# Squares of two RMS norms summed by TensorE, the normalised input split without being made, and 12 of the first 16 modulation tiles as matrix products with the weights moving

## The chip, the cores and the metric

The kernel runs on one core of one Trainium2 chip. A core has five engines that each work through their own list of instructions in order and wait for one another by semaphores: TensorE (PE, matrix products), VectorE (DVE), ScalarE (ACT), GpSimd (POOL) and SyncE (SP, which here only starts DMA transfers). The metric is the device time of one execution in microseconds (us).

## The reference, cut to what matters

Two blocks follow each other on 256 tokens of width 1024. The first has two layers; each runs a token mixer over 256 context tokens and 256 latent tokens, and then a PEER feed-forward layer. Both read a modulated RMS norm of the residual stream x:

```python
def rms_norm(x, g):
    y = xf * lax.rsqrt(jnp.mean(xf * xf, axis=-1, keepdims=True) + EPS)
    return (y * g)
def modulate(h, shift, scale):
    return h * (1 + scale) + shift
...
mod_x = (cond_x @ w_mod[l] + b_mod[l])      # 6 * 1024 values: shift, scale, gate, twice
hx  = modulate(rms_norm(x, norm1_g[l]), sh1x, sc1x)   # before the mixer: h @ w_in
hx2 = modulate(rms_norm(x, norm2_g[l]), sh2x, sc2x)   # before PEER: h @ wq (its queries)
```

The second block (feed-forward, retention and attention, feed-forward, twice) is not touched by the change.

## The kernel before, in words

x is kept transposed in SBUF: 128 partitions hold 128 channels, `x[:, k, :]` is the k-th of 8 channel blocks, and its 512 columns are the tokens (256 context, 256 latent). A projection is a sum over the 8 blocks; each f32 factor is cut in two parts, hi and lo (type fp32r), and three products replace one: hi·hi, lo·hi, hi·lo (`mm3`, L246 to L248). For weights, `Stream` fetches 512 KB tiles by DMA into six `raw` buffers; ScalarE writes `whi` (L209), VectorE or GpSimd `wlo` (L210). The order of the tiles is written out in `plan`, and SP issues their DMAs in that order: the seventh waits until the first buffer is free. `take` hands out the next tile; with `more` set it first splits further tiles, up to two ahead, as far as the buffers reach.

There are four norms of this kind: before the mixer of layer 0 (`mixer_start`), before PEER of layer 0, before the mixer of layer 1, and before PEER of layer 1 (the last with 256 tokens). Each goes so. `square_sum` squares one block of x on ScalarE and adds it to `nsum` on GpSimd or VectorE, block after block, as the residual (`resid`, L875) makes x. `norm_rstd` sums `nsum` over the partitions on TensorE (L333: for each 128 tokens a product with `nsum` as the stationary factor and a column of ones moving), takes the power -1/2 on GpSimd (L291) and spreads it over the partitions (L311, `n_pb`). `norm_tile` multiplies x by `n_pb` (VectorE, L346), writes `hhi` by ScalarE (L349) and the same value h in f32 by GpSimd or ScalarE (L353, L351), and VectorE takes `hlo` = h - `hhi` (L354). `norm_split` runs this block by block, with the first two projections behind each block.

At the start x comes in by DMA, and the first norm needs 16 modulation columns (8 scales, 8 shifts, for context and latent), each the product of a 512 KB tile of `w_mod` and the two condition vectors. `MODE` says who makes a tile: "T" (6 tiles) TensorE with the tile stationary and the two vectors moving, 8 products of 2 columns (L406); "V" (8 tiles) VectorE, two passes of 1024 elements with a running sum (L719); "G" (2 tiles) GpSimd and ScalarE (L714, L715).

PEER of layer 0 (`phase_v`) ends with eight PSUM banks `y`. `last(db)` adds what was gathered for 128 tokens by a product with the unit matrix (L1564), then comes the residual into x (L875) and the square for the next norm. In the output projection of a mixer, `proj` makes block m (24 products), then `resid`, `square_sum` and, in layer 0, one or two modulation tiles on VectorE.

Of the kernel before, what the change touches and what calls it, by code (L numbers as in the profile page):

```python
# [9 lines left out]
F32 = mybir.dt.float32  # L10
# [6 lines left out]
ALU = mybir.AluOpType  # L17
# [4 lines left out]
L = 2  # L22
# [84 lines left out]
def _host(inp):  # L107
# [8 lines left out]
    wt = g["w_mod"].reshape(L, KD, 128, 48, 128).transpose(0, 3, 2, 1, 4).reshape(L, 48, 128, 1024)  # L116
    wr = g["w_mod"].reshape(L, 1024, 48, 128).transpose(0, 2, 3, 1)
    a["w_modt"] = np.stack([(wt if MODE[i:i + 1] == "T" else wr)[l, m] for i, (l, m) in enumerate(MODT)])
# [120 lines left out]
class Build:  # L239
# [73 lines left out]
    def square_sum(self, pool, k, t0, eng=None, sq=None):  # L313

        nc, xk = self.nc, self.x[:, k, t0:]
        acc = self.nsum[:, t0:]
        if k == 0:
            nc.scalar.activation(acc, xk, AF.Square)
            return
        if sq is None:  # L320
            sq = pool.tile([128, 512], F32, name="n_sq", tag="n_sq", bufs=2)
        sq = sq[:, t0:]
# [3 lines left out]
    def norm_rstd(self, pool, psp, tag, t0):  # L326


        nb = (T - t0) // 128
        st = psp.tile([128, 512], F32, name="n_st", tag=tag)  # L330
        for tb in range(nb):
            s = slice(t0 + tb * 128, t0 + tb * 128 + 128)
            self.nc.tensor.matmul(st[:, tb:tb + 1], self.nsum[:, s], self.ones, start=True, stop=True)  # L333
        r = self.rsqrt_cols(pool, st[:, :nb], nb, 1.0 / 1024)
        pb = psp.tile([128, 512], F32, name="n_pb", tag=tag)
        for tb in range(nb):
            self.bcast(pb[:, tb * 128:tb * 128 + 128], r[:, tb:tb + 1])
        return pb

    def norm_tile(self, pool, k, pb, segs, t0, hhi, hlo, act=False):  # L340


        nc, N = self.nc, T - t0
        t, h = (pool.tile([128, w], F32, name="n_t", tag=g, bufs=2)
                for w, g in zip(self.norm_widths, ("n_t", "St")))
        nc.vector.tensor_mul(t[:, :N], self.x[:, k, t0:], pb[:, :N])  # L346
        for sl, g, sh in segs:
            ps = slice(sl.start - t0, sl.stop - t0)
            nc.scalar.activation(hhi[:, k, ps], t[:, ps], AF.Identity, scale=g(k), bias=sh(k))  # L349
            if act:  # L350
                nc.scalar.activation(h[:, ps], t[:, ps], AF.Identity, scale=g(k), bias=sh(k))  # L351
            else:
                nc.gpsimd.tensor_scalar(h[:, ps], t[:, ps], g(k), sh(k), op0=ALU.mult, op1=ALU.add)  # L353
        return lambda: nc.vector.tensor_sub(hlo[:, k, :N], h[:, :N], hhi[:, k, :N])  # L354

    def norm_split(self, pool, psp, tag, segs, t0, hhi, hlo, names, banks, ready=None):


        pb = self.norm_rstd(pool, psp, tag, t0)
# [16 lines left out]
    def mixer_start(self, p, pp, sp, hhi, hlo):  # L376
# [18 lines left out]
        segs = self.segs(0, 0, 0)  # L395

        def mods(k):
            mv = self.modv[0]
            src = [mv[:, 8 + k], mv[:, k]]
            for i in range(2):  # L400
                mode = MODE[2 * k + i]
                if mode == "T":
                    w = S.take(("modt", 2 * k + i), False)
                    src[i] = mo[:, 2 * k + i]
                    for kd in range(KD):
                        nc.tensor.matmul(src[i], w[:, kd * 128:kd * 128 + 128], cc[:, kd], start=kd == 0,  # L406
                                         stop=kd == KD - 1)
                else:
                    self.mod_tile(p, cb, 2 * k + i, "att" if mode == "G" else "sg", mode == "G", False)
            return src  # L410

        def gains(k, src):
            nc.vector.tensor_scalar(self.gsc[0][0][:, k], src[0], b1[:, k:k + 1],
                                    self.col["n1"][:, 0, k:k + 1], op0=ALU.add, op1=ALU.mult)
            nc.vector.tensor_scalar_add(self.modv[0][:, k], src[1], b[:, k:k + 1])

        made = {0: mods(0)}
        for k in range(KD):
            self.square_sum(p, k, 0, nc.vector)
        made[1] = mods(1)  # L420
        pb = self.norm_rstd(p, pp, "pp", 0)
        us = [S.take(("in", 0, j), False) for j in range(3)]
        nc.vector.tensor_scalar_add(b1, b[:, 8:16], 1.0)
        late = None
        for k in range(2, KD + 3):
            if k < KD:
                made[k] = mods(k)
            nxt = None
            if k - 2 < KD:
                gains(k - 2, made.pop(k - 2))  # L430
                nxt = self.norm_tile(p, k - 2, pb, segs, 0, hhi, hlo, True)
            if late:
                late()
                d = k - 3
# [78 lines left out]
    def plan(self):  # L513
# [1564 lines left out]
```

## Time and profile before

| | |
|---|---|
| time, median of 3 runs | 3865.55 us (3859.89 to 3867.29) |
| the profiled execution | 3849.67 us, of which its span 3847.7 us |
| busy: TensorE, VectorE, ScalarE, GpSimd | 95%, 75%, 49%, 31% of the span |
| chain that ended last: TensorE, VectorE, ScalarE, DMA | 74%, 13%, 5%, 3% of the span |
| last product of the first three projections issued | 74.44 us after the span's start |
| last column of the norm's sums, layer 0 to 1 (end of PEER) | 1675.54 us |

The first and the last instruction bound the span; the time holds about 2 us more. The profiled execution lies 16 us below the median of the runs. Busy shares are averages over stages; the chain follows, from the last instruction back, what released each step. The duration of a product contains its way through the array, so that two neighbours overlap: their pace is the distance of their starts.

### The profile page before, as it was taken

What the parts mean: (1) busy time and instruction counts of PE and PEld (TensorE: products, weight loads), DVE (VectorE), ACT (ScalarE), POOL (GpSimd) and SP (SyncE); (2) the same over time, 40 slices, a digit from 0 to 9 for tenths busy, and PEclk for the clock granted to TensorE, in tenths of its full rate; (3) what the DMA queues carried; (4) which work ended last, traced back from release to release, by engine and by line L of the source; (5) the groups of instructions that cost most, each with busy time, mean ns of one, the idle gap of its engine ahead of it and who ended that gap; (6) DMA issues with size and microseconds to landing.
All of it is one profiled execution on the core that took longest, in us unless ns stands there. A gap on an engine that the chain in (4) does not pass through costs nothing.

```text
span 3847.7 us, 67340 instructions
## 1 busy us (share of the span) xinstructions
PE 3662.7 (95%) x25755; PEld 3492.3 (91%) x25755; DVE 2893.2 (75%) x5232; ACT 1898.9 (49%) x3480; POOL 1181.2 (31%) x1126
## 2 busy tenths in 40 slices
PE   6898999999989999988899999999999999999999
PEld 5787799989889999978899999999999799998799
DVE  7977888898879999969687775876665566655555
ACT  5323347575744433343448685544445454444444
POOL 2433414343466676624470501212000300001300
PEclk9999999999999999989999999999999999999899
DMA  5423357989899999943366867878555255553254
GB/s 215 142 67 126 105 172 273 323 289 324 287 352 368 372 368 365 358 140 117 131 180 206 272 199 243 300 236 259 180 185 162 78 170 183 177 184 129 78 182 152
DMA packets 289121, 831.86 MB, mean 216 GB/s; under 512 B 32469, under 2 KB 98389, under 8 KB 287749
## 3 DMA queue, kind: packets, MB, share of 16 engines
q1 hardware_dynamic: 220782, 594.67, 46.7%
q0 software_dynamic: 67296, 231.65, 16.8%
q8 instruction: 201, 3.29, 0.4%
q10 hardware_dynamic: 720, 1.25, 0.1%
q14 instruction: 122, 1.00, 0.1%
HBM read 760.40 MB, written 67.04 MB: 215 GB/s over the span
## 4 chain that ended last, share of the span: by engine, by line
PE 74%; DVE 13%; ACT 5%; DMA 3%; issue 3%; POOL 2%; SPq 0%; DVEq 0%; ACTq 0%; POOLq 0%
PE ps L246 13%; PE ps L248 13%; PE ps L247 13%; PE y L246 9%; PE y L248 9%; PE y L247 9%; DVE wlo L210 3%; ACT whi L209 1%; DVE modt L719 1%; DMA x<-in_v_rows,eidx 1%; PE gp L1401 1%; POOL wlo L210 1%; DVE acc L1279 1%; PE gp L1402 1%; DMA raw<-in_w_modt 1%
## 5 line engine op out<-in xcount | busy, mean ns | idle before, releaser
L210 DVE TENSOR_TENSOR wlo<-raw,whi 128x1024 fp32r<-128x1024 f32 x884 | 1086.4, 1232 | 561.0 <-ACT whi L209 553.5
L209 ACT ACTIVATE whi<-raw 128x1024 fp32r<-128x1024 f32 x952 | 998.7, 1052 | 444.3 <-issue 178.5
L246 PE MATMUL ps<-hhi,whi 128*128 128x256 f32 (+1 forms) x3368 | 1026.8, 305 | 10.9 <-ACT hhi L349 5.3
L248 PE MATMUL ps<-hhi,wlo 128*128 128x256 f32 (+1 forms) x3368 | 1010.3, 300 | 13.9 <-DVE wlo L210 8.1
L247 PE MATMUL ps<-hlo,whi 128*128 128x256 f32 (+1 forms) x3368 | 1010.2, 300 | 4.9 <-DVE hlo L449 4.1
L246 PEld LDWEIGHTS ps<-hhi,whi 128*128 128x128 f32 x3368 | 656.2, 195 | 42.7 <-issue 9.9
L248 PEld LDWEIGHTS ps<-hhi,wlo 128*128 128x128 f32 x3368 | 655.1, 195 | 35.7 <-DVE wlo L210 11.7
L247 PEld LDWEIGHTS ps<-hlo,whi 128*128 128x128 f32 x3368 | 655.6, 195 | 27.5 <-DVE hlo L449 8.2
L246 PE MATMUL y<-wh,whi 128*128 128x256 f32 (+1 forms) x1280 | 374.7, 293 | 14.7 <-ACT wh L509 14.7
L248 PE MATMUL y<-wh,wlo 128*128 128x256 f32 (+1 forms) x1280 | 374.3, 292 | 0.6 <-DVE wlo L210 0.6
L247 PE MATMUL y<-wl,whi 128*128 128x256 f32 (+1 forms) x1280 | 374.6, 293 | 0.0
L246 PE MATMUL ps<-h2hi,whi 128*128 128x384 f32 x1024 | 350.2, 342 | 5.9 <-ACT scs L1115 4.9
L248 PE MATMUL ps<-h2hi,wlo 128*128 128x384 f32 x1024 | 344.7, 337 | 4.3 <-DVE wlo L210 4.3
L247 PE MATMUL ps<-h2lo,whi 128*128 128x384 f32 x1024 | 343.7, 336 | 0.0
L248 PE MATMUL y<-h2hi,wlo 128*128 128x384 f32 x768 | 257.5, 335 | 1.4 <-DVE wlo L210 1.2
L246 PE MATMUL y<-h2hi,whi 128*128 128x384 f32 x768 | 257.0, 335 | 0.0
L247 PE MATMUL y<-h2lo,whi 128*128 128x384 f32 x768 | 256.9, 334 | 0.0
L246 PEld LDWEIGHTS y<-wh,whi 128*128 128x128 f32 x1280 | 242.3, 189 | 15.2 <-ACT wh L509 15.2
L248 PEld LDWEIGHTS y<-wh,wlo 128*128 128x128 f32 x1280 | 242.2, 189 | 0.9 <-DVE wlo L210 0.9
L247 PEld LDWEIGHTS y<-wl,whi 128*128 128x128 f32 x1280 | 242.1, 189 | 0.5 <-DVE wl L510 0.5
L210 POOL TENSOR_TENSOR wlo<-raw,whi 128x1024 fp32r<-128x1024 f32 x68 | 174.5, 2579 | 213.1 <-ACT whi L209 212.9
L1202 ACT ACTIVATE act<-ps 128x384 f32<-128x384 f32 (+1 forms) x236 | 104.4, 442 | 262.3 <-PE ps L248 125.0
(448 smaller groups left out, 7576.4 us busy)
## 6 DMA issues: line engine op xcount, KB each, us to landing
raw<-in_pu SPq DMA_DIRECT2D x256, 512.0 KB
raw<-in_pv SPq DMA_DIRECT2D x256, 512.0 KB
raw<-in_ffn_gu SPq DMA_DIRECT2D x176, 512.0 KB
raw<-in_w_modt SPq DMA_DIRECT2D x96, 512.0 KB
raw<-in_w_in SPq DMA_DIRECT2D x88, 512.0 KB
raw<-in_ffn_dn SPq DMA_DIRECT2D x88, 512.0 KB
gd<-stage SPq DMA_DIRECT2D x48, 512.0 KB
actd<-act POOLq DMA_DIRECT2D x125, 192.0 KB
```

What stands on the lines that cost most here:

```text
L209: self.nc.scalar.activation(hi[:, :w], raw, AF.Copy)
L210: (self.lo_eng or self.nc.vector).tensor_sub(lo[:, :w], raw, hi[:, :w])
L246: mm(ps, whi, xhi, start=first, stop=False, **kw)
L247: mm(ps, whi, xlo, start=False, stop=False, **kw)
L248: mm(ps, wlo, xhi, start=False, stop=last, **kw)
L719: self.nc.vector.scalar_tensor_tensor(t, w, 1.0, cv, op0=ALU.mult, op1=ALU.mult, accum_out=acc)
L1202: nc.scalar.activation(act, ps[:, :N], AF.Gelu)
L1279: nc.vector.scalar_tensor_tensor(self.acc, v, c, self.acc, op0=ALU.mult, op1=ALU.add)
L1401: nc.tensor.matmul(ps[:, i], B[:, :, i], Ah[:, i], start=True, stop=False)
L1402: nc.tensor.matmul(ps[:, i], B[:, :, i], Al[:, i], start=False, stop=True)
```

## The change

- `square_sum` no longer adds on VectorE or GpSimd. It squares on ScalarE and returns `add`: for each 128 tokens a product with the square stationary and ones moving, summed over the 8 blocks in PSUM (`n_st`). In the output projections `add` of block m is called after `proj` of block m + 1, at the start and in `phase_v` at once. `norm_rstd` is called at the end of the stage that makes x, `norm_along` (the spreading) where it was.
- `norm_tile`: VectorE makes x · gain · `n_pb` in two halves of 256 columns, ScalarE adds the shift for `hhi`, and VectorE makes `hlo` = (t + shift) - `hhi` in two halves. h itself, and GpSimd's and ScalarE's part in it, are gone.
- At the start four scale tiles are "V" and twelve tiles are laid out so that the two condition vectors are stationary and the weights move: two products of 512 columns in plain f32 for a tile, four tiles for a group of four columns (`modp`), a copy by ScalarE (`modrow`) and four small transposes (`columns`). The V tiles are now taken with `more` at its default, True.
- The eight first modulation tiles stand ahead of the three `in` tiles in `plan` (four did).

```diff
-MODT = ([(0, m) for k in range(8) for m in (8 + k, k)] + [(0, m) for m in range(16, 48)]
-        + [(1, m) for m in range(48)])
+FIRST = [8, None, None, 9, None, None, 10, 11] + [None] * 8
+GROUPS = (0, 12, 4)
+MODT = [(0, m) for m in FIRST] + [(0, m) for m in range(16, 48)] + [(1, m) for m in range(48)]
-MODE = "TVTVGVTVTVGVTVTV"
...
-    def square_sum(self, pool, k, t0, eng=None, sq=None):
+    def square_sum(self, pool, st, k, t0, sq=None):
...
-        nc.scalar.activation(sq, xk, AF.Square)
-        (eng or (nc.vector if k == KD - 1 else nc.gpsimd)).tensor_add(acc, acc, sq)
+        nc.scalar.activation(sq[:, :T - t0], self.x[:, k, t0:], AF.Square)
+
+        def add():
+            for tb in range((T - t0) // 128):
+                nc.tensor.matmul(st[:, tb:tb + 1], sq[:, tb * 128:tb * 128 + 128], self.ones,
+                                 start=k == 0 and tb == 0, stop=k == KD - 1, skip_group_check=True)
+        return add
...
-    def norm_tile(self, pool, k, pb, segs, t0, hhi, hlo, act=False):
+    def norm_tile(self, pool, k, pb, segs, t0, hhi, hlo):
...
-        nc.vector.tensor_mul(t[:, :N], self.x[:, k, t0:], pb[:, :N])
+        for sl, ps, g, sh in cut:
+            nc.vector.scalar_tensor_tensor(t[:, ps], self.x[:, k, sl], g(k), pb[:, ps],
+                                           op0=ALU.mult, op1=ALU.mult)
+        for sl, ps, g, sh in cut:
+            nc.scalar.activation(hhi[:, k, ps], t[:, ps], AF.Identity, bias=sh(k))
+
+        def low():
+            for sl, ps, g, sh in cut:
+                nc.vector.scalar_tensor_tensor(hlo[:, k, ps], t[:, ps], sh(k), hhi[:, k, ps],
+                                               op0=ALU.add, op1=ALU.subtract)
+        return low
...
+        def mods(n):
+
+            if FIRST[n] is not None:
+                self.mod_tile(p, cb, n, "sg", False)
+                return
+            g, u = divmod(FIRST[:n].count(None), 4)
+            w = S.take(("modt", n), False)
+            if u == 0:
+                made[g] = g1.tile([128, 512], F32, name="modp", tag="g1")
             for i in range(2):
...
+                nc.tensor.matmul(made[g][:2], cc[:, 2 * u + i], w[:, i * 512:i * 512 + 512],
+                                 start=u + i == 0, stop=u + i == 4)
+            if u == 3:
+                nc.scalar.activation(row[:2, g], made[g][:2], AF.Copy)
...
+        mods(0)
...
         for k in range(KD):
...
+            self.square_sum(p, st, k, 0)()
+            if k in (1, 3):
+                mods(1 + k // 2)
+        mods(3)
+        mods(4)
+        self.norm_rstd(st, 0)
+        mods(5)
+        pb = self.norm_along(pp, "pp", 0)
+        columns(0)
+        mods(6)
+        mods(7)
         us = [S.take(("in", 0, j), False) for j in range(3)]
...
+                if k < 4:
+                    mods(8 + 2 * k)
+                    mods(9 + 2 * k)
+                    if k % 2:
+                        columns(1 + k // 2)
+                gains(k)
+                nxt = self.norm_tile(p, k, pb, segs, 0, hhi, hlo)
...
-                mods(0, 4)
+                mods(0, 8)
                 seq(w[:3], [("in", l, j) for j in range(3)])
-                mods(4, 12)
+                mods(8, 8)
...
                 self.proj(ps[:, :NQ], S.take(("out", l, m)), ochi, oclo, slice(0, NQ))
+                if add:
+                    add()
                 self.resid(l, 16, m, ps, t0)
-                self.square_sum(p, m, t0)
+                add = self.square_sum(p, nst, m, t0)
...
+                st = ys[0][:, 0]
                 for db in range(KD):
                     last(db)
-                    sq = self.stage[:, db % 2 * 4:db % 2 * 4 + 4].rearrange("p a b -> p (a b)")
-                    self.square_sum(v, db, 0, sq=sq)
+                    sq = self.stage[:, db * 4:db * 4 + 4].rearrange("p a b -> p (a b)")
+                    self.square_sum(v, st, db, 0, sq)()
+                self.norm_rstd(st, 0)
```

TensorE's list from its first product on; before, with two T tiles (L406) ahead of the sums:

```order
L406 MATMUL mod_124<-mod_75,raw 128x2 x16
L333 MATMUL n_st<-bones,nsum 128x1 x4
L311 MATMUL n_pb<-ident,rs_r 128x128 x4
L406 MATMUL mod_124<-mod_75,raw 128x2 x8
L246 MATMUL first_121<-hhi,whi 128x512
L247 MATMUL first_121<-hlo,whi 128x512
```

And the same place in the changed kernel:

```order
L326 MATMUL n_st<-bones,n_sq 128x1 x8
L414 MATMUL modp<-raw,mod_76 2x512 x2
L326 MATMUL n_st<-bones,n_sq 128x1 x8
L414 MATMUL modp<-raw,mod_76 2x512 x2
L326 MATMUL n_st<-bones,n_sq 128x1 x16
L414 MATMUL modp<-raw,mod_76 2x512 x4
L314 MATMUL n_pb<-ident,nr 128x128 x4
L421 MATMUL mod_125<-ident,modrow 128x2 x4
L414 MATMUL modp<-raw,mod_76 2x512 x8
L421 MATMUL mod_125<-ident,modrow 128x2 x4
L249 MATMUL first_122<-hhi,whi 128x512
```

The sums now stand between the modulation products, and two whole groups (16 products of 512 columns) stand ahead of the first projection's first product.

VectorE's list from its first V tile (L743, was L719) to the first block of the norm (L350), in the changed kernel:

```order
L743 SCALAR_TENSOR_TENSOR modt,mod_75<-raw,condb 128x1024 x2
L431 TENSOR_SCALAR gsc_79<-cols 128x8
L213 TENSOR_TENSOR wlo<-raw,whi 128x1024
L743 SCALAR_TENSOR_TENSOR modt,mod_75<-raw,condb 128x1024 x2
L333 TENSOR_SCALAR nm<-n_st 128x4
L213 TENSOR_TENSOR wlo<-raw,whi 128x1024
L743 SCALAR_TENSOR_TENSOR modt,mod_75<-raw,condb 128x1024 x4
L213 TENSOR_TENSOR wlo<-raw,whi 128x1024
L425 TENSOR_SCALAR gsc_77<-mod_75,gsc_79,cols 128x2
L427 TENSOR_SCALAR mod_75<-mod_125,cols 128x2
L350 SCALAR_TENSOR_TENSOR n_t<-x,gsc_77,n_pb 128x256 x2
```

The splits of the three `in` tiles (`wlo`), which stood together behind two V tiles, now stand one by one ahead of the second, the third and behind the fourth V tile.

TensorE's list at the end of PEER of layer 0 (`y0` to `y7` are the eight banks, `acc` the gathered part); before:

```order
L248 MATMUL y7_10711<-h2hi_2451,wlo_15877 128x384
L1564 MATMUL y0_10704<-ident_63,acc_3402 128x128
L1564 MATMUL y1_10705<-ident_63,acc_3402 128x128
L1564 MATMUL y2_10706<-ident_63,acc_3402 128x128
L1564 MATMUL y3_10707<-ident_63,acc_3402 128x128
```

And in the changed kernel, where `stage` holds the squares and the sums go to the first columns of `y0`:

```order
L251 MATMUL y7_10709<-h2hi_2466,wlo_15875 128x384
L1593 MATMUL y0_10702<-ident_63,acc_3400 128x128
L326 MATMUL y0_10702<-bones_66,stage_3763 128x1 x4
L1593 MATMUL y1_10703<-ident_63,acc_3400 128x128
L326 MATMUL y0_10702<-bones_66,stage_3763 128x1 x4
L1593 MATMUL y2_10704<-ident_63,acc_3400 128x128
```

The products with the unit matrix, which stood in one run, each have the four sums of the block before ahead of them, to the last (`y7`).

## Rows read from the trace of the kernel before

**Rows 1.** Page of the profile: the span, and the two halves of splitting a weight tile.

```profile
span 3847.7 us, 67340 instructions
...
L210 DVE TENSOR_TENSOR wlo<-raw,whi 128x1024 fp32r<-128x1024 f32 x884 | 1086.4, 1232 | 561.0 <-ACT whi L209 553.5
...
L209 ACT ACTIVATE whi<-raw 128x1024 fp32r<-128x1024 f32 x952 | 998.7, 1052 | 444.3 <-issue 178.5
```

**Rows 2.** Timeline of the start; columns: start us, length us, engine, line, operation.

```profile
9.06 1.23 DVE L719 SCALAR_TENSOR_TENSOR modt<-raw,condb 128x1024 f32<-128x1024 f32 x1 [8.19 <-ACT condb L701]
...
15.49 3.57 PE L406 MATMUL mod<-mod,raw 128*128 128x2 f32 x16 [7.22 <-DMA raw<-in_w_modt]
...
18.92 1.84 PE L333 MATMUL n_st<-bones,nsum 128*128 128x1 f32 x8
...
39.34 0.80 PE L247 MATMUL first<-hlo,whi 128*128 128x512 f32 x1 [3.86 <-DVE hlo L354]
...
39.94 0.63 PE L248 MATMUL first<-hhi,wlo 128*128 128x512 f32 x1
...
53.02 1.84 PE L406 MATMUL mod<-mod,raw 128*128 128x2 f32 x16
...
74.44 0.39 PE L248 MATMUL first<-hhi,wlo 128*128 128x512 f32 x1
```

**Rows 3.** Chain of work that ended last, start stage; columns: start us, length us, what.

```profile
40.57 0.43 PE first L246
...
92.15 3.44 DMA raw<-in_w_in
```

**Rows 4.** Timeline of TensorE in the second block, around one plain f32 product.

```profile
2989.19 1.02 PE L1831 MATMUL rp<-qk,rot 128*128 128x512 f32 x2
...
2990.17 0.28 PE L247 MATMUL ps<-hlo,whi 128*128 128x256 f32 x1
```

**Rows 5.** Timeline, end of the output projection of layer 0.

```profile
355.44 0.39 PE L248 MATMUL ps<-ochi,wlo 128*128 128x512 f32 x1
...
357.45 0.87 DVE L875 SCALAR_TENSOR_TENSOR x<-ps,mod,x 128x256 f32<-128x256 f32 x2
...
358.42 0.63 ACT L323 ACTIVATE n_sq<-x 128x512 f32<-128x512 f32 x1 [4.15 <-DVE x L875]
...
359.99 1.84 PE L333 MATMUL n_st<-bones,nsum 128*128 128x1 f32 x8 [4.16 <-DVE nsum L324]
...
362.11 1.96 POOL L291 TENSOR_TENSOR rs_r<-rs_m,neghalf 128x4 f32<-128x4 f32 x1 [1.85 <-DVE rs_m L289]
```

**Rows 6.** Windows, three stretches: length, busy PE, PEld, DVE, ACT, POOL, PEclk, DMA share, GB/s.

```profile
8.00:24.00 16.00, 6.51 (x30) 6.09 (x29) 12.66 (x19) 9.13 (x12) 2.95 (x2) 1.00 1.03 401
...
339.00:344.50 5.50, 5.50 (x26) 4.57 (x25) 5.50 (x8) 1.59 (x2) 1.42 (x1) 1.00 0.60 194
...
1662.00:1675.50 13.50, 3.77 (x26) 3.56 (x24) 7.05 (x17) 6.93 (x10) 7.59 (x6) 0.66 0.00 0
```

**Rows 7.** Timeline, end of the first PEER layer.

```profile
1662.02 1.95 PE L1564 MATMUL y<-ident,acc 128*128 128x128 f32 x16
...
1662.44 6.36 DVE L875 SCALAR_TENSOR_TENSOR x<-y,mod,x 128x256 f32<-128x256 f32 x16 [5.64 <-PE y L1564]
...
1663.35 0.63 ACT L318 ACTIVATE nsum<-x 128x512 f32<-128x512 f32 x1 [8.52 <-DVE x L875]
...
1664.13 0.63 ACT L323 ACTIVATE stage<-x 128x512 f32<-128x512 f32 x1 [0.15 <-DVE x L875]
...
1664.85 7.98 POOL L324 TENSOR_TENSOR nsum<-nsum,stage 128x512 f32<-128x512 f32 x6 [32.52 <-ACT stage L323]
...
1673.70 1.84 PE L333 MATMUL n_st<-bones,nsum 128*128 128x1 f32 x8 [9.73 <-DVE nsum L324]
```

**Rows 8.** Timeline, end of the output projection of layer 1.

```profile
1884.98 0.28 PE L248 MATMUL ps<-ochi,wlo 128*128 128x256 f32 x1
...
1887.05 0.48 DVE L875 SCALAR_TENSOR_TENSOR x<-ps,mod,x 128x256 f32<-128x256 f32 x1
```

More of the change, by code (lines that the diff above doesn't have):

```diff
@@ L335, in norm_rstd, with norm_along @@
+        return add
+    def norm_rstd(self, st, t0):
+        nc, nb = self.nc, (T - t0) // 128
+        nc.vector.tensor_scalar(self.nm[:, :nb], st[:, :nb], 1.0 / 1024, EPS, op0=ALU.mult, op1=ALU.add)
+        nc.gpsimd.tensor_tensor(self.nr[:, :nb], self.nm[:, :nb], self.neghalf[:, :nb], op=ALU.pow)
+    def norm_along(self, psp, tag, t0):
         pb = psp.tile([128, 512], F32, name="n_pb", tag=tag)
-        for tb in range(nb):
-            self.bcast(pb[:, tb * 128:tb * 128 + 128], r[:, tb:tb + 1])
@@ L338, in norm_rstd @@
-        return pb
-    def norm_tile(self, pool, k, pb, segs, t0, hhi, hlo, act=False):
-        nc, N = self.nc, T - t0
-        t, h = (pool.tile([128, w], F32, name="n_t", tag=g, bufs=2)
-                for w, g in zip(self.norm_widths, ("n_t", "St")))
-        nc.vector.tensor_mul(t[:, :N], self.x[:, k, t0:], pb[:, :N])
[L347 to L354, printed above, removed]
+        for tb in range((T - t0) // 128):
+            self.bcast(pb[:, tb * 128:tb * 128 + 128], self.nr[:, tb:tb + 1])
@@ new lines, in norm_along @@
+        return pb
+    def norm_tile(self, pool, k, pb, segs, t0, hhi, hlo):
+        nc = self.nc
+        t = pool.tile([128, self.norm_width], F32, name="n_t", tag="n_t", bufs=2)
+        cut = [(sl, slice(sl.start - t0, sl.stop - t0), g, sh) for sl, g, sh in segs]
+        for sl, ps, g, sh in cut:
[8 more added lines that the diff above has]
+        return low
@@ L414, in gains, with columns @@
+        def columns(g):
+            for i in range(4):
+                nc.tensor.transpose(mo[:, GROUPS[g] + i], row[:2, g, i * 128:i * 128 + 128], self.ident[:2, :2])
+        def gains(k):
+            sc = self.modv[0][:, 8 + k] if k < 4 else mo[:, 8 + k]
+            nc.vector.tensor_scalar(self.gsc[0][0][:, k], sc, b1[:, k:k + 1],
                                     self.col["n1"][:, 0, k:k + 1], op0=ALU.add, op1=ALU.mult)
-            nc.vector.tensor_scalar_add(self.modv[0][:, k], src[1], b[:, k:k + 1])
@@ L422, in mixer_start @@
+        mods(3)
[6 more added lines that the diff above has]
+        mods(7)
         us = [S.take(("in", 0, j), False) for j in range(3)]
-        nc.vector.tensor_scalar_add(b1, b[:, 8:16], 1.0)
         late = None
-        for k in range(2, KD + 3):
+        for k in range(KD + 1):
+            nxt = None
             if k < KD:
[L427 to L431, printed above, removed]
+                if k < 4:
[5 more added lines that the diff above has]
+                nxt = self.norm_tile(p, k, pb, segs, 0, hhi, hlo)
@@ L857, in mixer @@
                 cb = self.cond_rows(p, "cv")
+            nst, add = g1.tile([128, 512], F32, name="n_st", tag="g1"), None
             for m in range(8):
```

60 lines of the change are left out of this document (19 added, 41 removed).

## The prediction

> **What bounds the kernel now.** The time table comes first: TensorE is busy for 95% of the span and holds 74% of the chain that ended last, so most of the span is not touched by work on other engines. The change lies in four places where TensorE waits or might wait: the start, and the three later norms. I read each of them in the timeline, engine by engine, and let the windows say who is full.
>
> At the start TensorE is mostly late, not full: its last product of the first three projections starts at 74.44 us [rows 2], at 74.67 the next could follow. Two things are to be seen here. First, TensorE runs through its list in order: the product `lo·hi` waits 3.86 us for VectorE's `hlo`, and `hi·lo` behind it, whose factors were there, starts only after it, 39.34 and 39.94 [rows 2]. Second, the clock. Products of 512 columns follow each other in 0.43 us at 40.6 [rows 3], which is the 1.2 GHz level; the same kind of row takes half of that later, and 16 passes of a T tile took 3.57 us at 15.49 and 1.84 at 53.02 [rows 2]. The granted clock reads 1.00 from 8 to 24 us already [rows 6], so in this stretch I go by the rows' pace and not by that column.
>
> At the end of the output projection of layer 0 both TensorE and VectorE are full, 5.50 of 5.50 us [rows 6]; at the end of PEER of layer 0 neither is: of 13.5 us TensorE is busy 3.77 and VectorE 7.05 [rows 6], and GpSimd's six sums, 7.98 us in a row, hold the chain [rows 7].
>
> **Prices.** A column sum is, for 512 tokens, four products of one column, each in two passes. Eight such passes took 1.84 us [rows 2, 7] at 1.2 GHz; at 2.4 GHz a narrow pass takes 1.84/16 = 0.115 (the row at 53.02) [rows 2], so eight take 0.92. A plain f32 product of 512 columns does not occur at the start; the nearest rows are two passes at 2989.19, after which, with one product of 256 columns (0.12) between, the next starts at 2990.17 [rows 4]: 0.86 us. A moved modulation tile is two of these, 1.72 us at 2.4 GHz, and 3.44 at 1.2 (eight passes at the pace of 0.43 [rows 3]). That is what a T tile costs today, so TensorE has twelve times this where it had six, and no tile becomes cheaper there. A V tile is two passes of 1.23 us [rows 2], 2.46. Splitting a weight tile takes 1.05 on ScalarE and 1.23 on VectorE, 2.3 in all [rows 1]. A tile that is asked for when a buffer comes free lands 3.44 us later [rows 3]; a stream of them brings 512 KB in 1.3 us at 401 GB/s [rows 6].
>
> **The end of PEER of layer 0.** Before, eight unit products run ahead in one piece, the residuals follow on VectorE at 6.36/8 = 0.8 us a block, and the sums start at 1673.70 and end at 1675.54, 13.5 us after 1662.02 [rows 7]. Now unit product k + 1 stands behind the sums of block k. These wait for the square, that for the residual, and that for unit product k. So the eight blocks no longer overlap. One block: unit product to residual 0.42 (1662.02 to 1662.44), residual to square 0.91 (to 1663.35), square to its reader 0.72 (1664.13 to 1664.85), sums 0.92: 2.97 us at 2.4 GHz. At 1.2 GHz the sums take 0.92 more and the unit product about 0.2 more: 4.09. Which level? Today the granted clock over these 13.5 us is 0.66 [rows 6]; between 1.0 and 0.5 that is 4.3 us at 2.4 GHz, and then the sums run at half pace. TensorE will be as little busy, so I take 1.5 blocks at 2.97 and 6.5 at 4.09, 31.0 us: **+17.5**. Bounds: +10.2 with all blocks at 2.4 GHz (23.8 us), +19.2 with all at 1.2.
>
> **The output projection of layer 0.** GpSimd's sums leave, and with them whatever they take from VectorE; but TensorE was full as well, and gets 0.92 us more in each block from the third on. The sums of blocks 0 to 5 stand ahead of the last projection's end: +5.5. Behind it the chain is shorter: today from 355.83 (355.44 + 0.39) to the power at 362.11, 6.28 us [rows 5], as VectorE comes to the residual late (357.45). Now: residual at once 0.1, to the square 0.97, to the sums 0.72, sums 0.92, to the power 0.28 as today (361.83 to 362.11), 3.0 in all. 5.5 - 3.3 = **+2.2**; bounds +1.5 and +4 (sums at 1.2 GHz at the end).
>
> **The output projection of layer 1.** Four passes per block, 0.46 us, six blocks: TensorE ends 2.8 us later than 1885.26. But VectorE takes the last residual only at 1887.05 [rows 8], so 1.8 of that is covered by ScalarE and VectorE splitting weights; without this cover it would cost 2.8. The rest, 1.0, stands against VectorE's add and half of the sums, which go. **0**, bounds -0.5 and +1.5.
>
> **h split without being made.** Per block VectorE has four halves in place of two whole operations, at 0.40 each (6.36/16 [rows 7]) 1.6 us, and GpSimd none. TensorE's six products take 2.6 us at 1.2 GHz and 1.4 at 2.4; as these stretches begin at 1.2, VectorE gets ahead. **0** for the three later norms; if the clock rises early, at most 0.2 in each of 7 blocks is uncovered, +1.4 a norm, and half of GpSimd's wait at the first block may be gained.
>
> **The start.** Twelve products with moved weights, eight column sums and three transposed groups stand in TensorE's list, and the first projection's first product behind two whole groups. What decides is a ring: six buffers, in order. With TensorE at 2.4 GHz: the third tile lands at 15.49 and is used up at 17.2; its buffer receives the first `in` tile at 20.7; split, 22.9; only behind that split does VectorE take its second V tile, 25.4; that buffer receives the second `in` tile at 28.8; split 31.1; two V tiles 33.6 and 36.0; their buffers receive stream tiles that group two needs, 37.0 and 39.5; group done 42.9; copy and four transposes about 1.2, 44.1; first block of nine products 2.1, two tiles 3.4, second block 2.1, two tiles 3.4, columns 1.2, six blocks 12.4: 68.7. At 1.2 GHz up to the third tile, four sums cost 3.7 and two tiles 3.4 more: 75.8. Today's rows of this stretch are at 1.2 GHz, so I take the upper end, less what waits for landings hide: 74.7, **0** against today, bounds -6 and +5 (one more group at 1.2 GHz). VectorE and GpSimd lose six tiles' work between them, but VectorE's list now waits for splits that wait for buffers.
>
> **Sum.** 0 + 2.2 + 17.5 + 0 = +19.7 us. The profiled execution of 3849.67 would become 3869.4; it lies 15.9 below the median, so on the median 3865.55 the forecast is **3885**.
>
> **Rivals.**
> The clock stays at 2.4 GHz at the end of PEER, as the sums come every 3 us: +10.2 there, +12.4 in all, 3878. For it: TensorE is never idle for as long as today's 9.73 us [rows 7]. Against it: the granted 0.66 came with TensorE busy 28% of the stretch [rows 6].
> The start stays at 1.2 GHz through group two: +5, 3890. For it: today it still does at 40.6 [rows 3].
> The start is paced by DMA alone, which decides it for "not slower": 16 further tiles at 1.3 us after 15.49 end at 36.5; 1.7 for the last, 1.2 and 12.4 for the six blocks behind it give 51.8, a gain of 22.9 us and 3862 in all. It needs the second `in` tile's first product before some 30 us; against it stands the order of VectorE's list, where a split stands ahead of the second V tile.
> The column sums cost nothing, hidden behind weight loads of neighbours: blocks of 2.05, +2.9 at PEER, -4.2 and -0.4 at the projections, 3864. Against it: no narrow pass of these rows is under 0.115 [rows 2]. The Trainium skill, "TensorE: Matmul & The Clock Gate", section "Back-to-back issue gap", puts the floor for 1 to 64 columns at 25 ns, or 62 where decoding binds; with 62 a sum would take 0.50, and the whole change would be +6, 3872, as an estimate. The rows, 115 and 230 ns, do not agree: the stationary factor changes with every product.
> TensorE takes the next unit product ahead of waiting sums: then PEER costs about +3, 3871. Against it: 39.34 and 39.94 [rows 2]. The same page, section "Step-by-step: what each phase is for", says that only weight loads are pulled ahead and products keep their order; those two rows agree.
>
> **Chances.** Forecast 0.60, clock at 2.4 GHz 0.15, slow start 0.12, start paced by DMA 0.06, free sums 0.04, reordering 0.03. The range holds the first three with their bounds, 3869 to 3897. A measurement of this kernel can tell about 0.2%, 7.7 us, from no change. Slower by more: 0.87; within: 0.10; faster: 0.03, a part of the two cases near 3863 with a full clock at PEER.
>
> **What would show it.** At the end of PEER of layer 0, eight times unit product, residual, square, sums at 3 to 4 us; wrong if residuals still come every 0.8. In layer 0's projection, TensorE's blocks of 6.4 us instead of 5.5, VectorE with gaps. At the start, VectorE waiting for an `in` tile ahead of its second V tile, and the first projections ending between 69 and 80. The forecast fails if they end near 52, or if the sums at PEER show less than 0.1 us a pass.

## The result and the profile after

The changed kernel takes 3887.51 us (median of 8 runs, 3873.90 to 3898.17) where the kernel before, on the same chip, takes 3860.44. The ratio over all their runs is 1.0075 (the two medians alone give 1.0070), with a 95% interval of 1.0059 to 1.0092, that is 23 to 36 us slower. The forecast was 3885 us. Its difference, +19.7, is below that interval: of its terms the one for the start does not agree with the trace, the others do. That the time came so close is partly luck: the median of before is 5 us lower here than in the runs shown with the kernel. The profiled execution took 3898.17 us, the longest of the eight:

```profile
span 3896.3 us, 67525 instructions
```

Its span is 48.6 us longer than that of before [rows 1], some 20 more than the medians are apart. Three parts belong to the places of the change: 17.8 us at the start, 2.2 in the output projection of layer 0 and 17.7 at the end of PEER of layer 0, all three below. The other 11 us, 6.7 in PEER of layer 0 and 4.3 behind it, lie in stretches that differ as much between two executions of one kernel (last section).

**The end of PEER of layer 0.** Timeline of the changed kernel, from the first unit product (L1593) on, rows of five of its eight blocks:

```profile
1688.55 0.38 PE L1593 MATMUL y<-ident,acc 128*128 128x128 f32 x2
1688.97 0.88 DVE L904 SCALAR_TENSOR_TENSOR x<-y,mod,x 128x256 f32<-128x256 f32 x2 [5.64 <-PE y L1593]
1689.88 0.63 ACT L322 ACTIVATE stage<-x 128x512 f32<-128x512 f32 x1 [8.52 <-DVE x L904]
1690.56 1.05 PE L326 MATMUL y<-bones,stage 128*128 128x1 f32 x8 [1.63 <-ACT stage L322]
1691.47 0.47 PE L1593 MATMUL y<-ident,acc 128*128 128x128 f32 x2
...
1698.98 0.77 PE L1593 MATMUL y<-ident,acc 128*128 128x128 f32 x2
...
1703.11 0.77 PE L1593 MATMUL y<-ident,acc 128*128 128x128 f32 x2
...
1717.92 1.87 PE L326 MATMUL y<-bones,stage 128*128 128x1 f32 x8 [1.63 <-ACT stage L322]
```

Each unit product stands behind the sums of the block before it; the eight residuals that came every 0.8 us [rows 7] now come every 2.9 to 4.1. From 1688.55 to the end of the last sums, 1719.79, it is 31.2 us; before it was 13.5. In the six profiles with this order it is 31.2 to 32.3 us.

**The output projection of layer 0.** Timeline of its last two blocks in the changed kernel, and a window of 5.5 us in its middle and one in the PEER end (columns as in [rows 6]):

```profile
372.48 0.95 PE L326 MATMUL n_st<-bones,n_sq 128*128 128x1 f32 x8
...
378.64 0.39 PE L251 MATMUL ps<-ochi,wlo 128*128 128x512 f32 x1
378.87 0.95 PE L326 MATMUL n_st<-bones,n_sq 128*128 128x1 f32 x8
379.07 0.88 DVE L904 SCALAR_TENSOR_TENSOR x<-ps,mod,x 128x256 f32<-128x256 f32 x2 [1.66 <-PE ps L251]
...
382.09 1.95 POOL L334 TENSOR_TENSOR nr<-nm,neghalf 128x4 f32<-128x4 f32 x1 [48.73 <-DVE nm L333]
```

```profile
356.60:362.10 5.50, 5.50 (x30) 4.68 (x29) 3.40 (x8) 1.22 (x2) 0.00 (x0) 1.00 0.57 191
...
1698.98:1715.50 16.52, 10.00 (x41) 8.82 (x42) 3.50 (x8) 2.52 (x4) 0.00 (x0) 0.50 0.00 0
```

A block takes 6.39 us (372.48 to 378.87), the residual follows the last product at once, and VectorE is busy 3.40 of 5.50 us where it was full [rows 6]. In the PEER window the granted clock is 0.50, the 1.2 GHz level.

**The start.** Timeline of the changed kernel, rows of TensorE and one of VectorE:

```profile
16.67 3.55 PE L326 MATMUL n_st<-bones,n_sq 128*128 128x1 f32 x16 [16.67 <-DMA bones<-in_bones]
...
27.15 3.57 PE L414 MATMUL modp<-raw,mod 128*2 128x512 f32 x4
...
30.66 6.99 PE L326 MATMUL n_st<-bones,n_sq 128*128 128x1 f32 x32
...
35.93 1.23 DVE L213 TENSOR_TENSOR wlo<-raw,whi 128x1024 fp32r<-128x1024 f32 x1 [22.07 <-ACT whi L212]
...
50.16 9.76 PE L414 MATMUL modp<-raw,mod 128*2 128x512 f32 x16 [5.71 <-DMA raw<-in_w_modt]
...
92.22 0.39 PE L251 MATMUL first<-hhi,wlo 128*128 128x512 f32 x1
```

TensorE does nothing until 16.67 us, and what it waits for is `bones`, three columns of which the first is the ones, 1.5 KB by DMA. The list of DMAs of the first 20 us says how it comes so late (last column: us from issue to landing):

```profile
cols<-in_cols ACTq DMA_DIRECT2D x1, 121.0 KB, 6.5
ident<-in_ident ACTq DMA_DIRECT2D x1, 64.0 KB, 7.6
mod<-in_condc ACTq DMA_DIRECT2D x1, 8.0 KB, 3.3
bones<-in_bones ACTq DMA_DIRECT2D x1, 1.5 KB, 8.5
```

It is the last of ScalarE's loads, issued at 8.07 us. The three loads behind that of `mod` are issued so late because they stand in ScalarE's list behind its work on `condb`, which waits for a DMA until 7.19 us. The kernel before needed the ones first at 18.92, behind a T tile [rows 2], and so TensorE did not wait for them. From 16.67 on TensorE works through sums and tiles without a gap, at the 1.2 GHz pace up to about 42 us; then it waits 5.71 us for a tile of group two. The last product of the first projections is issued at 92.22 in place of 74.44: +17.8 us in this execution.

### The profile page after: what moved, and what is told of

Same layout as the page of the kernel before. It is cut to its first block, busy times and chain, and to the rows that moved or that the text cites. A ratio compares the mean times of both kernels' runs of the same rounds, so it can differ in the third digit from the quotient of the medians.

```text
span 3896.3 us, 67525 instructions
## 1 busy us (share of the span) xinstructions
PE 3716.6 (95%) x25915; PEld 3512.6 (90%) x25915; DVE 2868.9 (74%) x5254; ACT 1884.0 (48%) x3459; POOL 1124.3 (29%) x1064
## 4 chain that ended last, share of the span: by engine, by line
PE 66%; DVE 14%; issue 8%; DMA 6%; ACT 4%; POOL 3%; DVEq 0%; ACTq 0%; SPq 0%; POOLq 0%
PE ps L249 13%; PE ps L251 13%; PE ps L250 13%; PE y L249 6%; PE y L251 6%; PE y L250 6%; DVE wlo L213 3%; DMA vrow<-in_v_rows,eidx 2%; DMA x<-in_v_rows,eidx 2%; DVE acc L1308 1%; ACT whi L212 1%; DVE modt L743 1%; PE gp L1430 1%; POOL wlo L213 1%; PE modp L414 1%
## 5 line engine op out<-in xcount | busy, mean ns | idle before, releaser
L250 PEld LDWEIGHTS ps<-hlo,whi 128*128 128x128 f32 x3368 | 655.9, 195 | 29.3 <-DVE hlo L473 8.1
```

The lines of the kernel that those rows point to most:

```text
L250: mm(ps, whi, xlo, start=False, stop=False, **kw)
```

## Experiments

All start from the changed kernel unless another is named. At the end of PEER the theory was that the order of TensorE's list costs the time; its rival, that the passes of the sums do. At the start the theory was that TensorE's list sets the time, with the wait for the ones at its head; its rival, the ring of buffers, which the prediction had taken. There were twelve runs: ten versions, and both kernels once more. Ratios are to the kernel before on the same chip; a difference between two versions is the difference of their ratios, and it carries the uncertainty of both.

**Sums behind all residuals at the end of PEER.**

```diff
-                st = ys[0][:, 0]
+                st, adds = ys[0][:, 0], []
...
-                    self.square_sum(v, st, db, 0, sq)()
+                    adds.append(self.square_sum(v, st, db, 0, sq))
+                for add in adds:
+                    add()
```

> The changed kernel, but at the end of PEER of layer 0 the column sums come after all eight residuals: eight unit products, eight residuals and squares, then the 64 passes of the sums. Nothing is left out. Theory (order: unit product k + 1 stands behind sums that wait for block k's square): residuals again come every 0.8 us as in the kernel before (6.36 us for eight), and from the first unit product to the last sum the stage takes 9 us with TensorE at 2.4 GHz (last residual at about 7.1, square 0.7, sums 0.9) and 16.5 us at 1.2 GHz (64 passes of 0.23 us from 1.7 us on), in place of 31.2 in the changed kernel: 15 to 22 us less in all. Rival (the passes themselves, or their bank, are what is slow, and the order does not matter): the stage stays over 25 us, and the gain is under 6 us.

Measured: ratio to the kernel before 1.0027 (1.0016 to 1.0038), so 18.5 us less than the changed kernel by the difference of the ratios, uncertain by 8. Timeline of the stage:

```profile
1684.51 1.95 PE L1593 MATMUL y<-ident,acc 128*128 128x128 f32 x16
1684.93 6.36 DVE L904 SCALAR_TENSOR_TENSOR x<-y,mod,x 128x256 f32<-128x256 f32 x16 [5.64 <-PE y L1593]
...
1686.52 10.52 PE L326 MATMUL y<-bones,stage 128*128 128x1 f32 x64
...
1697.33 1.97 POOL L334 TENSOR_TENSOR nr<-nm,neghalf 128x4 f32<-128x4 f32 x1 [42.39 <-DVE nm L333]
```

The same 64 passes, 12.5 us from 1684.51 to 1697.04 in place of 31.2. Residuals follow each other in 0.8 us as before. The order was the cost, the passes were not: in the six profiles with the sums last the stage takes 11.05 to 13.90 us, no more than about what it took before the change (13.5).

**Ones without a DMA.**

```diff
-            self.ones = bones[:, 0:1]
+            self.ones = cp.tile([128, 1], F32, name="onec")
+            nc.vector.memset(self.ones, 1.0)
...
```

(Two small tiles of the norm are also put into one, which adds no instruction.)

> The changed kernel, but the column of ones is written in SBUF by VectorE at the program's begin instead of being taken from the three columns that a DMA brings. Nothing is left out. Theory (TensorE's list, in order, sets the start, and its first sums wait for that small transfer until 16.67 us): first sums at about 10.4 us, when the first square is there; the third modulation tile is used up at about 24.5 in place of 30.7 us, and the first three projections end at 86 to 87 in place of 92.45 us: 5.5 to 6.3 us less. Rival (the buffers' ring and the landings of tiles set it): the wait moves to a tile's landing, and the projections end within 2 us of 92.45.

Measured: 1.0054 (1.0037 to 1.0071), by the ratios 8 us less than the changed kernel, uncertain by 9, so that the time alone shows no gain. Timeline of TensorE:

```profile
10.40 3.57 PE L326 MATMUL n_st<-onec,n_sq 128*128 128x1 f32 x16 [10.40 <-ACT n_sq L322]
...
17.12 1.95 PE L326 MATMUL n_st<-onec,n_sq 128*128 128x1 f32 x16
...
37.93 8.36 PE L414 MATMUL modp<-raw,mod 128*2 128x512 f32 x16 [5.43 <-DMA raw<-in_w_modt]
```

The sums begin at 10.40 as the theory says. The first projections' last product is issued at 77.17, 15 us earlier, which is far more than the 6.3 of the wait and more than either expectation, since the pace also doubled at about 17 us already and not at 42. So one profile did not price the wait.

**The start of before**, with the rest of the change left in (its functions put back under other names; about 90 lines).

> The changed kernel with the start of the kernel before: its sums of squares on VectorE, its 6 T, 8 V and 2 G tiles, its order of tiles, its way to split h in this first norm; the three later norms stay as in the changed kernel. Nothing is left out. Theory (the start lost what its trace shows, and nothing of it is made good later): first projections end at 74.7 in place of 92.45 us, and the time falls by about 17.6 us. Rival (what comes late at the start is partly caught up behind it, for instance because fewer transfers or waits then stand in the way): the time falls by 10 us or less.

Measured: 1.0039 (1.0027 to 1.0052), 14 us less than the changed kernel, uncertain by 8; first projections' last product at 71.06. That lies between the two expectations and does not decide between them. From that product to the end of the span it takes 3804.6 us here and 3804.0 in the changed kernel, so these two profiles show nothing made good later; but three versions with the same program behind the start, those with the ones set, with early work and with V tiles not splitting ahead, take 3791.7 to 3802.1, so this is no proof. The 17.6 of the theory also rested on one profile of the changed kernel, and that was a late one (see its repetition below).

**V tiles without splitting ahead.**

```diff
-                self.mod_tile(p, cb, n, "sg", False)
+                self.mod_tile(p, cb, n, "sg", False, False)
```

> The changed kernel, but the four V tiles at the start are taken without splitting further tiles first. Nothing is left out. Theory of the prediction (the ring: VectorE's second V tile stands behind the first weight split, so buffers come free late, and group two's tiles land late): V tiles run as they land, VectorE's idle 22 us ahead of its first split is used, TensorE's wait of 5.7 us for group two's first tile goes, and the first projections end 4 to 6 us earlier, 86.5 to 88.5. Rival (TensorE's own list at 1.2 GHz sets the start; buffers that come free early help nothing, since SyncE issues the loads in order behind a buffer that TensorE frees late): within 2 us of 92.45.

Measured: 1.0066 (1.0048 to 1.0084), first projections' last product at 84.58. Timeline of TensorE:

```profile
24.25 1.95 PE L326 MATMUL n_st<-bones,n_sq 128*128 128x1 f32 x16
...
27.93 4.21 PE L326 MATMUL n_st<-bones,n_sq 128*128 128x1 f32 x32
...
42.26 9.95 PE L414 MATMUL modp<-raw,mod 128*2 128x512 f32 x16 [2.61 <-DMA raw<-in_w_modt]
```

Beside the first profile the end is 7.6 us earlier, as the prediction's ring would have it, and the wait for group two's tile fell from 5.71 to 2.61. But here the pace also rose at 24.3, not 42 us. The next run tells how much of the 7.6 each of the two was.

**The changed kernel again.**

> The changed kernel once more, unchanged. Its first profile showed TensorE at the 1.2 GHz pace from its first sum at 16.67 to 42 us, and the run without early splits, whose sums began 0.6 us later, a rise at 24.3. Theory (the moment of the first rise differs between executions of one kernel, and with it the end of the start): over many runs the times spread by some 20 us, and a profile whose rise comes near 24 ends its first projections near 85 in place of 92.45 us. Rival (the rise belongs to the kernel): again 42 and 92 us.

Measured: 1.0074 (1.0051 to 1.0097), 3867.54 to 3891.12. Timeline of TensorE:

```profile
16.09 3.55 PE L326 MATMUL n_st<-bones,n_sq 128*128 128x1 f32 x16 [16.09 <-DMA bones<-in_bones]
19.57 3.57 PE L414 MATMUL modp<-raw,mod 128*2 128x512 f32 x4
23.07 1.95 PE L326 MATMUL n_st<-bones,n_sq 128*128 128x1 f32 x16
...
26.76 4.20 PE L326 MATMUL n_st<-bones,n_sq 128*128 128x1 f32 x32
...
43.80 8.60 PE L414 MATMUL modp<-raw,mod 128*2 128x512 f32 x16 [5.33 <-DMA raw<-in_w_modt]
...
83.35 0.39 PE L251 MATMUL first<-hhi,wlo 128*128 128x512 f32 x1
```

Sixteen passes take 3.55 us and then 1.95: the rise, here at 23.07, with the same program. From the third tile used up to the last product it takes 83.35 - 26.76 = 56.6 us here, and 84.58 - 27.93 = 56.7 with the V tiles taken without splitting ahead. So that edit alone brought the end no earlier, as its rival said (its 92.45 is the end with the late rise); the 7.6 us were the rise. The ring's wait was there all the same: 5.33 us against 2.61. What the edit won there, group two lost, 9.95 us against 8.60, and so did the first block behind it, whose products follow each other in 0.43 us there and in 0.23 here. Whether that slower pace came with the edit or with the execution is open: the first profile has the long wait, 9.76 us for group two and the 0.43.

**The kernel before again.**

> The kernel before once more, unchanged, for a second profile. Theory (the stretch from 772 to 1655 us, PEER of layer 0 with its gathers, took 3 to 7 us longer in all five later profiles than in the first one, 882.8 us, because that one execution was quick): 886 to 890 us here too. Rival (the change lengthens it): again within 1.5 us of 882.8.

Measured: 3849.53 us, and 884.9 us for that stretch. It lies between the two expectations: see the last section. This profile also has what the first one of this kernel lacks, the landing of the ones (the second row is from the list of DMAs, its last column as above):

```profile
8.28 0.45 ACTq L390 DMA_DIRECT2D bones<-in_bones  x1
...
bones<-in_bones ACTq DMA_DIRECT2D x1, 1.5 KB, 7.8
...
19.22 1.84 PE L333 MATMUL n_st<-bones,nsum 128*128 128x1 f32 x8
```

They land at about 16.1 us here too, 3 us before TensorE first reads them.

**Both places undone**: the start of before, and the sums last at PEER.

> The changed kernel with two parts undone: the start of the kernel before, and at the end of PEER of layer 0 the column sums behind all eight residuals. What stays of the change: sums by TensorE and h split without being made in the three later norms. Nothing is left out. Theory (the losses lie in those two places, and they add up): what is left is +2.7 us in the output projection of layer 0, -1.0 at the end of PEER, about 0 elsewhere, so the time is the kernel before's within 4 us (3856 to 3864). Rival (part of the loss is spread over the rest, as in PEER's gathers, which were longer in every profile with the change): 5 to 10 us slower than before.

Measured: 3856.68 against 3855.92, ratio 1.0004 (0.9993 to 1.0015). So the loss lies in these two places: undone together they give back 27 us. Undone one by one they gave 18.5 and 14, together 32, which agrees within an uncertainty of 10.

**Early work for TensorE** (with the ones set).

```diff
...
+        nc.gpsimd.memset(row[:, 0], 0.0)
+        for i in range(10):
+            nc.tensor.matmul(ps[i % 3], row[:, 0, :128], row[:, 0], start=True, stop=True)
...
```

> The changed kernel with the column of ones written by VectorE and, ahead of the first sums, ten plain f32 products of 512 columns on a zeroed tile into a bank that is written anew later; nothing is left out. TensorE would otherwise be idle until 10.4 us. Theory (at the start TensorE's list is the bound, so its clock decides: earlier work brings the rise earlier): the 2.4 GHz pace is there by 12 us in place of 16.8 and 42 us, the eight sums and two tiles are done 4 to 5 us earlier than with the ones alone, and the first projections end at 71 to 75 us. Rival (the landings of tiles and VectorE's splits are the bound once the ones are early): the end stays within 2 us of 77.4.

Measured: 1.0077 (1.0054 to 1.0100), no better than the changed kernel. Timeline of TensorE:

```profile
1.31 11.42 PE L431 MATMUL first<-modrow 128*128 128x512 f32 x20 [1.31 <-POOL modrow L429]
12.57 1.84 PE L326 MATMUL n_st<-onec,n_sq 128*128 128x1 f32 x16
...
35.77 9.44 PE L414 MATMUL modp<-raw,mod 128*2 128x512 f32 x16 [5.63 <-DMA raw<-in_w_modt]
```

The rise came, and sums and tiles were done early; yet the first projections' last product is issued at 77.78. What is won ends in the wait for group two's tile, 5.63 us, and after it products again stand at half pace. The rival's number holds, and in this profile the next wait is a landing.

**Ones set, V tiles without splitting ahead, sums last at PEER** (the edits above together).

> The changed kernel with three edits: the column of ones written by VectorE, the four V tiles taken without splitting ahead, and the sums at the end of PEER of layer 0 behind all residuals. Nothing is left out. Theory (once the ones are early, the ring of buffers is the next bound: with the ones alone TensorE still waits 5.4 us for group two's first tile): that tile no longer queues behind the loads of two weight tiles, lands some 3 us earlier, and the first projections end at 73.5 to 75.5 in place of 77.4 us, if TensorE's pace rises at about 17 us as there; time about 3 us over the kernel before (0 to +6). Rival (the V tiles' place changes nothing, as in the run with that edit alone, which ended 1.2 us later than the repeated changed kernel with a rise 1.2 us later): 77 to 78 us.

Measured: first projections' last product at 73.19, the wait for group two's tile 3.3 us in place of 5.4, as the theory has it. The time, 1.0023 (1.0013 to 1.0033), is not: 9 us over the kernel before. The profiled execution, 3854.84 us, is the quickest of ten, and seven of them took 3860.95 to 3869.48; so the profile shows the good case only.

**Four tiles moved ahead in TensorE's list**, on top of the last.

```diff
+        mods(1)
         for k in range(KD):
             self.square_sum(p, st, k, 0)()
-            if k in (1, 3):
-                mods(1 + k // 2)
-        mods(3)
-        mods(4)
+            if k == 1:
+                mods(2)
+                mods(3)
+                mods(4)
+            if k == 3:
+                mods(5)
         self.norm_rstd(st, 0)
-        mods(5)
```

> As the run before it, and at the start the products of four tiles are moved ahead in TensorE's list: the first ahead of all sums, the second and third behind two sums, the fourth behind four; nothing is left out. Theory (TensorE frees the buffers; what it consumes late lands late for group two): the fourth tile is used up at 24 to 27 in place of 31 us, group two's first tile lands before TensorE asks for it, its wait of 5 us goes, and the first projections end at 69 to 73 us; time at most that of the kernel before (-4 to +3). Rival (sums come later, and with them n_pb and the whole norm, so the gain is lost there): 75 us or more.

Measured: 1.0001 (0.9990 to 1.0012), without one of the eleven executions, which took 11492.65 us. The wait for group two's tile is down to 0.4 us, but the last product is issued at 74.36, between the two expectations: n_pb waits 2.3 us for GpSimd and the sums 1.2 us for a square. The time is the theory's, and 8.5 us under the version before it, uncertain by 6.

**Output projection of layer 0 with its old sums**, on top of the version with both places undone.

```diff
-                add = self.square_sum(p, nst, m, t0)
+                if l == 0:
+                    self.square_sum0(p, m, t0)
+                else:
+                    add = self.square_sum(p, nst, m, t0)
...
```

> The version with the start of the kernel before and the sums last at the end of PEER, and in the output projection of layer 0 the sums of squares are again made on GpSimd and VectorE. Nothing is left out. Theory (TensorE was full in that projection, so 64 further passes there cost their own time): the stretch from the weight split at 340.0 to that at 384.0 us takes 44.0 us again in place of 46.7 to 47.3, and the time falls by 2.7 us against that version, to 0 to 3 us under the kernel before. Rival (the sums on TensorE cost nothing and the 2.7 us come from h split in halves): still 46 us or more.

Measured: 3847.88 against 3853.72, ratio 0.9987 (0.9976 to 0.9998). The window over that stretch:

```profile
344.30:388.00 43.70, 35.53 (x145) 28.18 (x144) 35.07 (x72) 16.55 (x32) 7.02 (x6) 0.84 0.39 133
```

From VectorE's split at 344.33 to GpSimd's first at 388.04 it is 43.7 us (44.0 in the kernel before, from 339.98 to 384.03), where the version without this edit takes 47.3 and the changed kernel 46.7. That window begins at a split, and VectorE can split ahead by more or less; TensorE's own rows give less. From the projection's first product to the spreading of the norm (`n_pb`) they take 56.0 us here (312.38 to 368.39) and 56.1 in the kernel before, 57.0 without this edit and 58.5 in the changed kernel. So the profile shows 1.0 us for this edit; by the times it is 6.6, uncertain by 6, and what the rest is stays open. This is the only version whose interval lies below the kernel before, by 0.8 to 9 us, and only just. Of the change it keeps h split without being made in the three later norms, and TensorE's sums at the end of PEER (last) and in layer 1.

**The changed kernel's start, mended, with the rest of that version.**

> The version that the runs point to: the changed kernel's start with the column of ones written by VectorE, V tiles without splitting ahead and four tiles moved ahead in TensorE's list; in the output projection of layer 0 the sums on GpSimd and VectorE as before; at the end of PEER of layer 0 the sums behind all residuals. Nothing is left out. Theory (terms add up): start -2 to -5 against the kernel before, out projection 0, PEER -1, layer 1 -1: 3851 to 3856 where the kernel before has 3856 to 3860, a gain of 3 to 6 us, which 12 runs can just tell. Rival (the start's pace is a matter of when the clock rises, and its mean is no better than before): within 2 us of the kernel before.

Measured: 0.9999 (0.9984 to 1.0015); 3838.91 to 3867.11. This is the rival: the mended start is not shown to be better than the old one in the mean (4.6 us slower than the version above, uncertain by 7), and it varies more, 28 us over 12 executions against 20 over 35 of the kernel before.

## Why the prediction came out as it did

- **End of PEER, +17.5: right.** 31.2 us against 31.0 forecast. Blocks of 2.92, 3.38 and then 4.13 us stand against 2.97 and 4.09; the granted clock is 0.50 in the later blocks. The rival with 2.4 GHz throughout falls with that window, the one with reordering with the rows at 1691.47 and 1703.11, which start where the sums end.
- **Free sums: refuted.** Eight passes took 1.05 us at 2.4 GHz and 1.87 at 1.2 there. The estimate of 62 ns per pass, from the Trainium skill, "TensorE: Matmul & The Clock Gate", section "Back-to-back issue gap", gave 3872; no run here shows such a pass with a new stationary factor each time.
- **Output projection of layer 0, +2.2: right.** Blocks of 6.39 us against 6.4; from the last product's end (378.64 + 0.39) to the power at 382.09 it is 3.06 against 3.0. The power comes 19.98 us later than before [rows 5], of which 17.78 are the start's: 2.2. From the projection's first product to `n_pb` TensorE's rows take 58.5 and 58.6 us in the two profiles of the changed kernel, 56.1 and 56.4 in the two of the kernel before.
- **Output projection of layer 1 and h split, 0: right.** From `n_pb` ahead of layer 1's mixer to `n_pb` behind its output projection it took 213.8 and 212.8 us before, 213.4 and 213.2 after.
- **The start, 0: the step that failed.** The step is "the third tile lands at 15.49 and is used up at 17.2", with "four sums cost 3.7 and two tiles 3.4 more" at 1.2 GHz, which is 24.3. In the first profile, at 1.2 GHz up to there, it was used up at 30.66, 6.4 us later, and 6.3 is what the sums wait for the ones (16.67 against 10.40 with the ones set). The step had priced every product and the landing of every tile, and left out the landing of the smallest operand; the profile of before that it went by lists that load's issue and no landing. The term was mis-sized a second time farther on. From the third tile to the end of group two the chain has 25.7 us (17.2 to 42.9), and 29.3 and 25.6 were measured; from there to the end it has 25.8, and 32.3 and 30.9 were measured, with two waits for `hlo` of 1.45 us and products at half pace, where the chain had none of either. By the difference of the ratios the start cost +14 us, uncertain by 8. With the changed start the last product of the first projections is issued at 92.22, 83.35 and 91.62 in three profiles (the last with the sums last at PEER), with the old one at 71.06 to 75.27 in five. The bounds were -6 and +5, and the sign that was named, an end between 69 and 80, did not come.
- **The rivals for the start.** Paced by DMA alone falls: the end is not near 52. The slow start, +5, is seen in part: the pace was 1.2 GHz up to about 42 us and again at first in group two in one profile, but only up to 23 us in the other; it too left out the ones.
- **The ring.** That a split stands ahead of VectorE's second V tile is seen (the row at 35.93, 22.07 us of idle time), and it made TensorE wait: 5.71 and 5.33 us for group two's tile, 2.61 without splitting ahead. But the ring was not where the loss came from, and that edit alone brought the end no earlier.
- **A reading that was wrong without effect.** A moved tile is four passes of about 0.88 us at 1.2 GHz (3.57 us for x4 at 27.15), not eight of 0.43; the price, 3.44, holds.

With +14 in place of 0 the sum would have been +33.7, and 23 to 36 were measured. With the start undone 15 us remain (10 to 20), where the other terms of the forecast give 19.7.

## What to carry to other kernels

When a change makes something start earlier, list every operand of it, constants too, and find out when each lands: in the trace of before a late landing makes nobody wait as long as its first reader is later still, and it may not even be listed. Where only the issue is listed, give the landing a term with bounds. On an engine that runs its list in order, a small product that waits for a round through two other engines must not stand between products that feed that round; behind them the same 64 passes cost next to nothing here. And when a start depends on when the clock rises, one profile of each kernel is not enough to compare their starts: two of one kernel differed by 8.9 us.

## What the runs showed that was not expected

- The moment of TensorE's first rise to the 2.4 GHz pace belongs to the execution. In two kernels with the same start the first sums began at 16.14 and 16.09 us, and TensorE worked without a gap from there; the pace rose at about 41.5 us in the one (sums last at PEER) and at 23.1 in the other (the changed kernel again). Up to the rise the granted clock reads 1.00 in both; only the rows' pace tells. What decides it, no row here shows.
- A load of 1.5 KB took 8.5 us to land, as the third on its queue behind 121 and 64 KB, while SyncE's queue moved some 400 GB/s; one of 8 KB on the same queue, issued at 0.74 us before that stream was up, took 3.3. In the other profiles that list it the small load took 7.8 to 8.2. The Trainium skill, "DMA: Bandwidth & Descriptors", section "Queues, rings and completion order", says that the engines take turns between queues by packet; by that a second queue gets its share under a stream, but not the right of way. A landing that is late but comes while the stream still runs agrees with this; how much of the 8.5 us are such turns, no row shows, and no run here moved that load or its issue.
- PEER of layer 0 from the split at 772.09 us in the kernel before to that at 1654.86, which the change doesn't touch, took 882.7 to 895.3 us in fourteen profiles (882.8 and 884.9 in the kernel before, 889.5 and 895.3 in the changed one, 882.7 in the fastest version). From the end of its sums to the end of the span it is 2162.6 to 2176.9 us in them (2172.2 and 2170.0 in the kernel before, 2176.5 and 2169.7 in the changed one). With 6.7 and 4.3 us of these and 8.9 of the late rise, the first profiled pair is further apart than the medians. Whether any of the longer PEER comes from the change stays open; the version with both places undone shows no such remainder in its time.
